# A third group of four outputs by seven products in the second SwiGLU, with the weight sums issued at listed chunks

## The chip, the cores and the metric

The kernel runs on one core of one Trainium2 chip. Its time is device time in microseconds (us) of one execution; shown are the median of several runs and, for the profile, one execution taken by the hardware profiler.

## The reference

Two decoder layers over 256 tokens of 1024 features, all in float32. Layer 0 is a short gated convolution, a cross-attention to 256 memory tokens, and a SwiGLU; layer 1 is a block-sparse causal attention that reads keys and values made once from layer 0's output, the same kind of cross-attention, and a SwiGLU. Before each part stands an RMS norm, behind each a residual sum. The change is in the SwiGLU:

```python
def swiglu(h, w_gu, w_down):
    g, u = jnp.split(h @ w_gu, 2, axis=-1)
    return (jax.nn.silu(g) * u) @ w_down
```

with h of 256 x 1024, w_gu of 1024 x 5632 and w_down of 2816 x 1024. Its 2816 outputs are worked on as 11 pairs (jp = 0 to 10) of two times 128.

## The kernel before, in words

**Precision.** Every float32 operand is split into a high and a low part (hi, lo) of a shorter type, and a product is three matmuls: hi by lo, lo by hi, hi by hi. Activations are split when they are made. Weights come from DRAM in chunks of 128 x 1024 (512 KB): a load on the SP queue into one of RAWS = 5 buffers (raw), a copy on ACT that makes hi, a subtraction on DVE that makes lo, into one of WBUFS = 10 pairs of buffers. Loads, copies and subtractions run ahead of the matmuls in one fixed order of chunks, the plan that weight_plan() returns; class Feed walks along it. A chunk's load is issued when the chunk five before it has been subtracted; its copy needs the chunk ten before it to be used up.

**The order of everything** is made when the kernel is built: PE's matmuls are written down in program order, and small jobs (generators) are put in between by a model of the engines' times (Clock, Side). The order is then fixed on each engine.

**The SwiGLU (swiglu).** The first two pairs are made by rows, the others two ways:
- A plain pair (gate_up): for each of the two outputs, gate and up are each 8 matmuls of 128 x 512 and 8 of 128 x 256 (tile gu), and ACT and DVE turn them into one output (tile guT). After each output come two blocks of the down product (tile ff, 6 matmuls each) of the pair two before.
- A group of two pairs by seven products (seven(jp), which makes jp and jp + 1). Tokens are cut into two halves, features into two halves, and gate and up are the two halves of the outputs: a 2 x 2 by 2 x 2 product. It is made by Winograd's form of Strassen's method, with seven products of 12 matmuls (tile seven) in place of eight. It needs sums over the tokens' halves (S1 to S4, made once per layer by token_sums) and sums of quarters of the weights (T1 to T4). After each product stands one block of the down product, after the last two. The results of the first token half (u0) and the second (p5) are turned by four PE transposes each (tile pt_g) and split into guT. product() takes one of two PSUM tiles for each product.

GROUPS lists the jp of the groups by layer: before, 8 in layer 0, 4 and 8 in layer 1.

**The weight sums** are made in DRAM by DMAs alone (sum_steps), 16 steps a group, two halves each: T1 is a copy of quarter B11, T3 a copy of B12, then B12 is added to T1 and B22 to T3, T2 is a copy of T1 with B22 added, T4 a copy of T2 with B21 added. Copies are issued on SP's queue, in which the weight loads stand too; additions are accumulating DMAs on GpSimd's queue (POOL), which also makes the rs (the power of -1/2) of each norm. A step waits for the one that it builds on, and whatever stands behind it in its queue waits with it. SUMS_AT says at which chunk of the plan a step is put into its queue: before, the steps of a layer were spread evenly from a first to an end chunk. In program order the chunks are, in layer 0: memv 40 to 47, mq 48 to 55, mo 56 to 63, SwiGLU 64 to 135; then k, q, v 136 to 159, memk 160 to 167, o 168 to 175, memv 176 to 183, mq 184 to 191, mo 192 to 199, and layer 1's SwiGLU from 200 on. A chunk is loaded some ten chunks before it is used.

Names in the profile: L464 is every matmul, L468 every transpose, L242 every instruction of ACT, DVE and POOL, L481 the loads, L551 and L553 the additions and the copies of the weight sums. raw_w, hi_w and lo_w are weight chunks: wr the row pairs, wg and wu gate and up of a plain pair, wB and wT quarters and sums of a group, wd the down weights; hn is a normed half of the tokens, pt_h its transposes.

Of the kernel before, what the change touches and what calls it, by code (L numbers as in the profile page):

```python
# [42 lines left out]
SPARE = 1500  # L43
LATER = 2000
BANKWISE = 5
GROUPS = ((8,), (4, 8))
SUMS_AT = ((44, 104, 104), (128, 220, 210))


class Rows:  # L50
# [18 lines left out]
def weight_plan():  # L69
# [61 lines left out]
    def ffn_plan(l):  # L131
        steps, last = ffn_steps()
        plan = []
        for kind, jp in steps + [("down", jp) for jp in last]:
            if kind == "gu" and jp in GROUPS[l]:
                plan += seven_plan(l, jp)
            elif kind == "gu" and jp - 1 in GROUPS[l] or kind == "down" and \
                    any(jp + ROW_PAIRS - g in (0, 1) for g in GROUPS[l]):
                pass
# [32 lines left out]
    for l in range(2):  # L172
        for jp in GROUPS[l]:
            for name in QUARTER:
# [224 lines left out]
def yoco_kernel(  # L399
# [22 lines left out]
    vector, scalar, pool = (Timed(clock, n, e) for n, e in  # L422
                            (("dve", nc.vector), ("act", nc.scalar), ("pool", nc.gpsimd)))
    side = Side(clock, tp=2, gu=2, half=HALVES, pair=PAIRS)
# [8 lines left out]
    def tp_tile(name):  # L433
        return ps_tp.tile([P, 4, P], F32, tag="tp", name=name)
# [21 lines left out]
    def tok(h):  # L456
        return slice(h * P, (h + 1) * P)
# [9 lines left out]
    def transpose(o, i):  # L467
        nc.tensor.transpose(o, i, ident[:i.shape[0], :i.shape[0]])  # L468
        clock.note("pe", 109, [o], [i], 200)
# [65 lines left out]
    def sum_steps(l, jp):  # L535
        for name in ("T1", "T2", "T3", "T4"):
            for i in range(2):
                weight_sums[l, jp, name, i] = aside.tile([P, 2, 2 * T], F32, name=f"{name}_{l}_{jp}_{i}")

        def step(name, source, i, add):  # L540
            dst = weight_sums[l, jp, name, i]
            if source[0] == "T":
                src = weight_sums[l, jp, source, i]
            else:
                n = quarters[l, jp, source, i]
                src = chunks[n * P:(n + 1) * P].rearrange("p (a n) -> p a n", a=2)

            def run():
                clock.free["dma"] = max(clock.free["dma"], clock.now)
                if add:  # L550
                    nc.gpsimd.dma_start(dst, src, accum_op=OP.add, max_dma_last_dim=8192)  # L551
                else:
                    nc.sync.dma_start(dst, src)  # L553
                clock.note("dma", 3300 if add else 1460, [], [])

            return run

        order = (("T1", "B11", False), ("T3", "B12", False), ("T1", "B12", True), ("T3", "B22", True),
                 ("T2", "T1", False), ("T2", "B22", True), ("T4", "T2", False), ("T4", "B21", True))
        return [step(name, source, i, add) for name, source, add in order for i in range(2)]  # L560

    plan, _, quarters, ffn_steps = weight_plan()
    feed = side.feed = Feed(clock, plan, load_chunk, split_high, split_low)
# [71 lines left out]
    def split_steps(hi, lo, pt, kind="tp"):  # L635
        scalar.copy(hi, pt)
        yield
        vector.tensor_sub(lo, pt, hi)
        side.give(kind)
        yield  # L640
# [398 lines left out]
        feed.hooks[36 + k] = [put_aside(k)]  # L1039

    for l in range(2):
        steps = [step for jp in GROUPS[l] for step in sum_steps(l, jp)]
        first, end, last = SUMS_AT[l]
        for n, step in enumerate(steps):
            at = min(first + (end - first) * n // len(steps), last + n - len(steps))
            feed.hooks.setdefault(at, []).append(step)


    def short_conv(act, into):
# [179 lines left out]
    def swiglu(l, src, done, fine_end=False, at_end=None):  # L1229
        act = src.act  # L1230
        guT = Act(side, [])

        def unit_of(j):
            if j // 4 == len(guT.units):
                guT.units.append(acts.tile([P, 4, 2, T], F32R, tag="unit", name=f"guT{l}_{j // 4}"))
            return guT.units[j // 4], j % 4
# [121 lines left out]
        def seven(jp):  # L1358

            u, j0 = unit_of(2 * jp)  # L1360
            bank_jobs, t = {}, {}
# [93 lines left out]
            def turn_parts4(src, h):  # L1455
                yield from side.hold("tp")
                pt = tp_tile("pt_g")
                for i in range(4):
                    transpose(pt[:, i, :], src[:, i * P:(i + 1) * P])
                side.give("half")  # L1460
                yield
                yield from split_steps(u[:, :, 0, tok(h)], u[:, :, 1, tok(h)], pt)

            EVICT = {"B11": b11, "B21": b21, "T1": t1, "T3": t3, "T2": t2, "B22": b22, "T4": t4}
            n = jp - ROW_PAIRS
# [17 lines left out]
                next_down()  # L1483
            next_down()
            for h, name in enumerate(("B22", "T3")):
                guT.add_job(h, jp // 2, bank_jobs[name])

        def down_w(jp):
            return [feed.take(f"wd{l}_{2 * jp + i}") for i in range(2)]
# [14 lines left out]
        steps, last = ffn_steps()  # L1504
        sums_job = [side.start(token_sums())]
        for jp in range(ROW_PAIRS, NP):
            if jp in GROUPS[l]:
                seven(jp)
# [3 lines left out]
            n = jp - ROW_PAIRS  # L1512
# [248 lines left out]
```

## Time and profile before

| | |
|---|---|
| median of 3 runs | 783.08 us (783.0 to 783.8) |
| the profiled execution | 783.51 us, of which the span from the first to the last instruction 781.7 |
| granted TensorE clock | 0.998 |
| PE busy | 773.4 us (99%), 4147 matmuls |
| DVE, ACT, POOL busy | 573.6 (73%), 458.8 (59%), 36.8 (5%) |
| moved by DMA | 182.71 MB, 234 GB/s |

Times in the trace count from the start of the span. A row of the chain gives its start, its length, and what it is; a row of a group gives how many instructions, their busy time and the mean in ns of one, then the idle time of the engine ahead of them; a row of a window gives the busy time of PE, PEld (weight loads of PE), DVE, ACT and POOL, PE's granted clock, the mean share of the 16 DMA engines, and GB/s. Layer 1's SwiGLU runs from 594.74 us to the end of the span.

### The profile page before, as it was taken

Reading aid. Unit: us, or ns where it says so; the run is one execution under the profiler, and the core shown is the slowest. Engines: PE = TensorE matmul, PEld = TensorE weight load, DVE = VectorE, ACT = ScalarE, POOL = GpSimd, SP = SyncE. Lnnn points to the kernel's source line nnn. Section 1 sums busy time; section 2 is a strip of 40 time slices with the busy share of each in tenths; the row PEclk is TensorE's granted clock in tenths of the full one; section 3 lists DMA queues with packets and bytes.
Section 4 is the critical chain, followed back from the end, with each engine's and each line's share of the span. In section 5 each row is a group of like instructions: output and inputs, shape, how many; then the busy total and the mean of one; then the engine's idle time right before and its main releaser. Section 6 shows DMA issues by size and latency. Waiting matters only on the chain.

```text
span 781.7 us, 11230 instructions
## 1 busy us (share of the span) xinstructions
PE 773.4 (99%) x4147; PEld 665.0 (85%) x4147; DVE 573.6 (73%) x872; ACT 458.8 (59%) x728; POOL 36.8 (5%) x68
## 2 busy tenths in 40 slices
PE   9999999999999999999999999999999999999996
PEld 8988888898888888888888889888988888888885
DVE  6988888768786566687766566876867876966964
ACT  6875665665654555566564563655756556655741
POOL 1000011000100000000110010030000000000000
PEclk9999999999999999999999999999999999999999
DMA  9776888916676755699787556899674646946931
GB/s 345 277 275 214 275 287 230 372 67 212 193 245 232 226 174 205 207 366 330 217 306 243 188 161 218 294 266 310 208 224 151 241 158 226 321 164 211 345 111 54
DMA packets 48807, 182.71 MB, mean 234 GB/s; under 512 B 6256, under 2 KB 7280, under 8 KB 46576
## 3 DMA queue, kind: packets, MB, share of 16 engines
q1 hardware_dynamic: 45968, 166.79, 59.7%
q0 software_dynamic: 2208, 14.68, 9.2%
q8 instruction: 32, 0.52, 0.3%
q10 hardware_dynamic: 576, 0.52, 0.2%
q14 instruction: 23, 0.19, 0.1%
HBM read 178.82 MB, written 28.31 MB: 265 GB/s over the span
## 4 chain that ended last, share of the span: by engine, by line
PE 95%; DVE 1%; issue 0%; ACT 0%; POOLq 0%; DVEq 0%; ACTq 0%
PE gu L464 17%; PE ff L464 15%; PE seven L464 7%; PE q_acc L464 6%; PE cu L464 6%; PE rows L464 6%; PE acc_mo L464 6%; PE acc_memv L464 6%; PE acc_memk L464 4%; PE pb L464 3%; PE acc_v L464 3%; PE acc_q L464 3%; PE acc_o L464 3%; PE acc_cout L464 3%; PE acc_k L464 3%; PE po L464 2%
## 5 line engine op out<-in xcount | busy, mean ns | idle before, releaser
L464 PE MATMUL ff<-hi_wd,guT 128*128 128x512 f32 (+1 forms) x352 | 108.2, 388 | 0.0
L464 PEld LDWEIGHTS ff<-hi_wd,guT 128*128 128x128 f32 x352 | 65.8, 188 | 12.8
L464 PE MATMUL ff<-lo_wd,guT 128*128 128x512 f32 (+1 forms) x176 | 68.3, 388 | 0.0
L242 DVE TENSOR_TENSOR gu_sb<-gu_sb,gu 128x256 f32<-128x256 f32 x48 | 19.9, 421 | 58.7 <-ACT gu_sb L242 58.0
L242 DVE TENSOR_TENSOR lo_wd<-raw_wd,hi_wd 128x1024 fp32r<-128x1024 f32 x44 | 53.5, 1221 | 2.9 <-ACT hi_wd L242 2.7
L242 ACT COPY gu_sb<-gu 128x256 f32<-128x256 f32 x48 | 17.8, 372 | 61.4 <-PE gu L464 61.3
L242 ACT CAST hi_wd<-raw_wd 128x1024 fp32r<-128x1024 f32 x44 | 46.1, 1050 | 11.3 <-DMA raw_wd<-in_chunks_dram 9.4
L464 PE MATMUL gu<-ffn,hi_wg 128*128 128x512 f32 x192 | 48.0, 390 | 0.0
L464 PE MATMUL gu<-ffn,hi_wu 128*128 128x512 f32 x192 | 47.6, 390 | 0.0
L464 PE MATMUL acc_memk<-mT,hi_memk 128*128 128x256 f32 x256 | 44.3, 291 | 0.0
L242 ACT CAST hi_wu<-raw_wu 128x1024 fp32r<-128x1024 f32 x32 | 33.5, 1051 | 15.2 <-DMA raw_wu<-in_chunks_dram 10.9
L464 PEld LDWEIGHTS gu<-ffn,hi_wg 128*128 128x128 f32 x192 | 35.9, 188 | 7.3
L464 PEld LDWEIGHTS gu<-ffn,hi_wu 128*128 128x128 f32 x192 | 35.8, 188 | 7.3
L464 PE MATMUL rows<-hi_wr,ffn 128*128 128x512 f32 x128 | 40.7, 395 | 0.0
L464 PE MATMUL acc_mo<-hi_mo,oT_mem 128*128 128x512 f32 x128 | 40.6, 393 | 0.0
L464 PE MATMUL acc_memv<-hi_memv,mT 128*128 128x512 f32 x128 | 39.6, 390 | 0.0
L242 DVE TENSOR_TENSOR lo_wu<-raw_wu,hi_wu 128x1024 fp32r<-128x1024 f32 x32 | 38.9, 1221 | 0.6 <-ACT hi_wu L242 0.5
L464 PEld LDWEIGHTS acc_memk<-mT,hi_memk 128*128 128x128 f32 x256 | 38.8, 199 | 0.4 <-ACT hi_memk L242 0.3
L464 PEld LDWEIGHTS ff<-lo_wd,guT 128*128 128x128 f32 x176 | 33.2, 188 | 6.2
L242 POOL TENSOR_TENSOR rs<-ms,neg_half 128x1 f32<-128x1 f32 x14 | 13.5, 964 | 436.6 <-DVE ms L242 420.2
L464 PE MATMUL q_acc<-mem,hi_mq 128*128 128x512 f32 x128 | 32.4, 394 | 0.0
L242 DVE TENSOR_TENSOR lo_wg<-raw_wg,hi_wg 128x1024 fp32r<-128x1024 f32 x24 | 28.7, 1221 | 4.0 <-ACT hi_wg L242 3.9
(277 smaller groups left out, 1954.6 us busy)
## 6 DMA issues: line engine op xcount, KB each, us to landing
raw_wd<-in_chunks_dram SPq DMA_DIRECT2D x44, 512.0 KB, 4.9
raw_wu<-in_chunks_dram SPq DMA_DIRECT2D x32, 512.0 KB, 5.0
T<-in_chunks_dram POOLq DMA_DIRECT2D x24, 512.0 KB, 7.6
raw_wg<-in_chunks_dram SPq DMA_DIRECT2D x24, 512.0 KB, 5.0
raw_wT<-T SPq DMA_DIRECT2D x24, 512.0 KB, 4.7
raw_wB<-in_chunks_dram SPq DMA_DIRECT2D x18, 512.0 KB, 5.0
raw_memv<-in_chunks_dram SPq DMA_DIRECT2D x16, 512.0 KB, 4.7
raw_mq<-in_chunks_dram SPq DMA_DIRECT2D x16, 512.0 KB, 6.0
```

The lines of the kernel that those rows point to most:

```text
L242: return call(out, *args, **kw)
L464: nc.tensor.matmul(o, l, r, start=start, stop=stop)
```

## The change

GROUPS gets three groups in layer 1, at 3, 6 and 8 (pairs 3 and 4, 6 and 7, 8 and 9; plain are 2, 5 and 10). SUMS_AT becomes a list of 16 chunks for each group, in the order of the steps. A group that begins at an odd pair has its outputs in two tiles of guT, so the last split goes in two halves, and the job that others wait for is entered under both tiles.

```diff
-GROUPS = ((8,), (4, 8))
-SUMS_AT = ((44, 104, 104), (128, 220, 210))
+GROUPS = ((8,), (3, 6, 8))
+SUMS_AT = {
+    (0, 8): (65,) * 8 + (74, 77, 81, 85, 89, 92, 96, 100),
+    (1, 3): (101, 103, 104, 106, 107, 109, 110, 111, 128, 131, 134, 137, 140, 143, 146, 149),
...
+}
@@
     for l in range(2):
-        steps = [step for jp in GROUPS[l] for step in sum_steps(l, jp)]
-        first, end, last = SUMS_AT[l]
-        for n, step in enumerate(steps):
-            at = min(first + (end - first) * n // len(steps), last + n - len(steps))
-            feed.hooks.setdefault(at, []).append(step)
+        for jp in GROUPS[l]:
+            for at, step in zip(SUMS_AT[l, jp], sum_steps(l, jp)):
+                feed.hooks.setdefault(at, []).append(step)
@@
-                yield from split_steps(u[:, :, 0, tok(h)], u[:, :, 1, tok(h)], pt)
+                if j0 == 0:
+                    yield from split_steps(u[:, :, 0, tok(h)], u[:, :, 1, tok(h)], pt)
+                    return
+                for i, v in enumerate((u, unit_of(2 * jp + 2)[0])):
+                    c, q = slice(2 - 2 * i, 4 - 2 * i), pt[:, 2 * i:2 * i + 2, :]
+                    scalar.copy(v[:, c, 0, tok(h)], q)
+                    yield
+                    vector.tensor_sub(v[:, c, 1, tok(h)], q, v[:, c, 0, tok(h)])
+                side.give("tp")
+                yield
@@
-                guT.add_job(h, jp // 2, bank_jobs[name])
+                for g in sorted({jp // 2, (jp + 1) // 2}):
+                    guT.add_job(h, g, bank_jobs[name])
```

The two groups at 6 and 8 follow each other without a plain pair in between. The steps of the group at 6 stand at chunks 159 (T1 with its additions), 166 (T3 with its additions) and 174 to 194; of the group at 8 at 168 (the copies of T1 and T3 and the additions to T1), 201 to 203 and 206 to 209.

What this moves on PE, at the third pair of layer 1. Before, behind the last down block of pair 0 (ff1_1_1 with wd1_1) stands the plain pair 3:

```order
L464 MATMUL ff1_1_1_6306<-hi_wd1_1_6208,guT1_0_6147 128x512 x2
L464 MATMUL gu_6468<-ffn1_0_6014,hi_wg1_3_0_6256 128x512 x4
L464 MATMUL gu_6468<-ffn1_1_6015,hi_wg1_3_1_6267 128x512 x4
L464 MATMUL gu_6487<-ffn1_0_6014,hi_wu1_3_0_6286 128x512 x4
L464 MATMUL gu_6487<-ffn1_1_6015,hi_wu1_3_1_6293 128x512 x4
L464 MATMUL gu_6468<-ffn1_0_6014,lo_wg1_3_0_6257 128x256 x4
L464 MATMUL gu_6468<-ffn1_1_6015,lo_wg1_3_1_6268 128x256 x4
L464 MATMUL gu_6487<-ffn1_0_6014,lo_wu1_3_0_6287 128x256 x4
L464 MATMUL gu_6487<-ffn1_1_6015,lo_wu1_3_1_6294 128x256 x4
L464 MATMUL ff1_0_0_6303<-lo_wd1_2_6439,guT1_0_6147 128x512
```

In the changed kernel the first product of the group at 3 stands there (B11 is a quarter of the weights; the rows left out repeat the two before them for the other row block of the chunk):

```order
L469 MATMUL ff1_1_1_6330<-hi_wd1_1_6232,guT1_0_6171 128x512 x2
L469 MATMUL seven_6490<-lo_wB11_1_3_0_6281,ffn1_0_6038 128x512
L469 MATMUL seven_6490<-hi_wB11_1_3_0_6280,ffn1_0_6038 128x512 x2
...
L469 MATMUL seven_6490<-lo_wB11_1_3_1_6292,ffn1_0_6038 128x512
L469 MATMUL seven_6490<-hi_wB11_1_3_1_6291,ffn1_0_6038 128x512 x2
...
L469 MATMUL ff1_0_0_6327<-lo_wd1_2_6311,guT1_0_6171 128x512
```

32 matmuls of a plain output, half of them 256 wide, have given way to 12 of 512, and the down block behind them is one instead of two.

The end of a group on PE. Before, behind the group at 4, the transposes of p5 stand after two down blocks and seven matmuls of the plain pair 6:

```order
L464 MATMUL ff1_1_1_6306<-hi_wd1_7_6714,guT1_1_6309 128x512 x2
L464 MATMUL gu_6895<-ffn1_0_6014,hi_wg1_6_0_6786 128x512 x4
L464 MATMUL gu_6895<-ffn1_1_6015,hi_wg1_6_1_6801 128x512 x3
L468 MATMUL pt_g_6907<-ident_95,p5_6720 128x128 x4
L464 MATMUL gu_6895<-ffn1_1_6015,hi_wg1_6_1_6801 128x512
```

Now there are two such ends in the middle: behind the group at 3 a plain pair follows, behind the group at 6 the first product of the group at 8 (the two pieces stand one below the other):

```order
L469 MATMUL ff1_1_1_6330<-hi_wd1_5_6589,guT1_1_6333 128x512 x2
L469 MATMUL gu_6769<-ffn1_0_6038,hi_wg1_5_0_6661 128x512 x4
L473 MATMUL pt_g_6778<-ident_95,p5_6595 128x128 x4
L469 MATMUL gu_6769<-ffn1_1_6039,hi_wg1_5_1_6676 128x512 x4
...
L469 MATMUL ff1_1_1_6330<-hi_wd1_11_7021,guT1_2_6730 128x512 x2
L469 MATMUL seven_7200<-lo_wB11_1_8_0_7094,ffn1_0_6038 128x512
L469 MATMUL seven_7200<-hi_wB11_1_8_0_7093,ffn1_0_6038 128x512 x2
...
L469 MATMUL seven_7200<-lo_wB11_1_8_1_7109,ffn1_0_6038 128x512
L473 MATMUL pt_g_7212<-ident_95,p5_7027 128x128 x4
L469 MATMUL seven_7200<-hi_wB11_1_8_1_7108,ffn1_0_6038 128x512 x2
```

The transposes behind the group at 3 have moved forward by three matmuls; behind the group at 6 seven matmuls stand ahead of them as before.

On SP's queue, the last sums of the group at 8 and the row blocks of layer 1's SwiGLU (mo1 are the last weights of the attention to memory, wr1 the row blocks). Before:

```order
L481 DMA raw_mo1_4_5489<-in_chunks_dram 128x1024
L553 DMA T2_1_8_0_513<-T1_1_8_0_511 16x8192
L481 DMA raw_mo1_5_5506<-in_chunks_dram 128x1024
L481 DMA raw_mo1_6_5550<-in_chunks_dram 128x1024
L553 DMA T2_1_8_1_514<-T1_1_8_1_512 16x8192
L481 DMA raw_mo1_7_5585<-in_chunks_dram 128x1024
...
L481 DMA raw_wr1_1_1_5876<-in_chunks_dram 128x1024
L553 DMA T4_1_8_0_517<-T2_1_8_0_513 16x8192
L481 DMA raw_wr1_1_2_5910<-in_chunks_dram 128x1024
L553 DMA T4_1_8_1_518<-T2_1_8_1_514 16x8192
```

and in the changed kernel:

```order
L486 DMA raw_wr1_0_1_5736<-in_chunks_dram 128x1024
L558 DMA T2_1_8_0_521<-T1_1_8_0_519 16x8192
L558 DMA T2_1_8_1_522<-T1_1_8_1_520 16x8192
L486 DMA raw_wr1_0_2_5798<-in_chunks_dram 128x1024
L486 DMA raw_wr1_0_3_5813<-in_chunks_dram 128x1024
L486 DMA raw_wr1_1_0_5877<-in_chunks_dram 128x1024
L486 DMA raw_wr1_1_1_5918<-in_chunks_dram 128x1024
L558 DMA T4_1_8_0_525<-T2_1_8_0_521 16x8192
L486 DMA raw_wr1_1_2_5928<-in_chunks_dram 128x1024
L558 DMA T4_1_8_1_526<-T2_1_8_1_522 16x8192
```

T4 has kept its place; T2, on which it waits, has moved back to four loads ahead of it. On GpSimd's queue the additions to T4 stand, as before, directly ahead of the two rs of the last norm.

2 rows, old and new, of the table SUMS_AT are left out of this document.

## Prediction

> **What bounds the kernel now.** I read the page's busy times and chain first, then the waits of PE, then the pieces of the chain around a group of seven products, then the windows of the stretches in which the change adds work. The page says that one engine is busy from end to end:
>
> ```profile
> span 781.7 us, 11230 instructions
> PE 773.4 (99%) x4147; PEld 665.0 (85%) x4147; DVE 573.6 (73%) x872; ACT 458.8 (59%) x728; POOL 36.8 (5%) x68
> PE 95%; DVE 1%; issue 0%; ACT 0%; POOLq 0%; DVEq 0%; ACTq 0%
> ```
>
> A busy PE alone proves little, since matmuls overlap; that it waits for nobody is told by its list of waits, which has two rows in the whole execution:
>
> ```profile
> PE warm L464 <- DVE blank L763: 1.5, 1, 1.5
> PE acc_memk L464 <- DVE lo_memk L242: 0.4, 1, 0.4
> ```
>
> So between the start and the last matmul PE is the path. Work taken off PE shortens the kernel by what it took, work added on any other engine costs nothing as long as PE still finds its operands ready. Both halves of the change can be read that way.
>
> **What the change takes off PE.** These are pieces of the chain in the second layer: one pair of outputs the plain way, the group of two pairs by seven products that begins at 651.94, and the start of the next plain pair (start, us, what).
>
> ```profile
> 635.36 5.54 PE gu L464 x32
> 640.90 2.75 PE ff L464 x12
> ...
> 651.94 2.72 PE seven L464 x12
> ...
> 678.19 0.44 PE pt_g L468 x4
> ...
> 682.79 1.59 PE gu L464 x7
> 684.38 0.44 PE pt_g L468 x4
> ```
>
> A plain pair takes 651.94 - 635.36 = 16.58 us, its down products included, so two pairs take 33.16. The group, which does the same two pairs with the same down products, takes 682.79 - 651.94 = 30.85 us with its first four transposes, and the second four (0.44) fall into the next pair: 31.29. One group more saves 33.16 - 31.29 = 1.87 us of PE time. The layer goes from five plain pairs and two groups to three plain pairs and three groups, so that is the whole gain on PE. Sums over the tokens (S1 to S4) are made once per layer already and are not made again.
>
> **What it adds elsewhere, and why I cost it at about nothing.** First the splitting of weights on ACT and DVE. A group needs 14 blocks of weights and sums and 4 down blocks, 18 in all, where two plain pairs need 12. The new order puts two groups back to back, 36 blocks in 62.6 us, one in 1.74 us. What the feed can do is seen in the group of before: its window, and the splits that DVE did in it.
>
> ```profile
> 651.90:683.30 31.40, 31.40 (x140) 25.62 (x139) 29.04 (x32) 22.61 (x25) 0.00 (x0) 1.00 0.89 318
> L242 DVE TENSOR_TENSOR lo_wT<-raw_wT,hi_wT 128x1024 fp32r<-128x1024 f32 x8 | 9.4, 1222 | 1.2 <-ACT hi_wT L242 1.2
> L242 DVE TENSOR_TENSOR lo_wd<-raw_wd,hi_wd 128x1024 fp32r<-128x1024 f32 x4 | 4.9, 1222 | 0.3 <-ACT hi_wd L242 0.3
> L242 DVE TENSOR_TENSOR lo_wB<-raw_wB,hi_wB 128x1024 fp32r<-128x1024 f32 x4 | 4.8, 1221 | 0.0
> L242 DVE TENSOR_TENSOR lo_wu<-raw_wu,hi_wu 128x1024 fp32r<-128x1024 f32 x2 | 2.4, 1222 | 0.0
> L242 DVE TENSOR_TENSOR lo_wg<-raw_wg,hi_wg 128x1024 fp32r<-128x1024 f32 x2 | 2.4, 1218 | 0.0
> ```
>
> DVE (third busy time, 29.04 of 31.40) made 8 + 4 + 4 + 2 + 2 = 20 blocks, one in 1.57 us, two more than the group used up, while PE was busy all of 31.40. Without those two DVE would be busy 29.04 - 2 x 1.22 = 26.6 us per group. Two groups in a row therefore still gain on the demand. They also start with a lead, for the blocks that the second group will need first stand where wg stands now:
>
> ```profile
> 671.84 2.35 DVE L242 TENSOR_TENSOR lo_wg<-raw_wg,hi_wg 128x1024 fp32r<-128x1024 f32 x2
> 680.07 0.69 DVE L242 TENSOR_TENSOR m<-seven,m 128x512 f32<-128x512 f32 x1
> 680.79 0.69 DVE L242 TENSOR_TENSOR p<-p,m 128x512 f32<-128x512 f32 x1
> 681.40 1.22 DVE L242 TENSOR_TENSOR lo_wd<-raw_wd,hi_wd 128x1024 fp32r<-128x1024 f32 x1
> 682.54 0.68 DVE L242 TENSOR_TENSOR p<-p,m 128x512 f32<-128x512 f32 x1
> 684.22 0.60 PE L468 MATMUL pt_g<-ident,p 128*128 128x128 f32 x4
> ```
>
> They are ready at 674.19 and wanted at 682.79, 8.6 us ahead. Cost: 0, and the bound above is the second rival.
>
> Second, the seams. The same rows show the one handover that PE takes with little to spare: after the last product p goes through four DVE rows, done at 683.22, and its transposes run at 684.22, a spare 1.0 us. PE fills that time with two down blocks and seven matmuls of the next output. At the seam between the second and third group the order keeps seven matmuls, the same spare. Behind the first group only four stand there; three fewer at 1.59 / 7 = 0.23 us each leave 0.3 us. Cost between 0 and, if one more split of 1.22 us gets in between, 0.9 + 0.2 us; I take 0.1, since the number of splits between those rows is the same in the new order. An odd first pair also makes its results land in two tiles, so an eviction of 512 columns becomes two of 256: a few tenths on ACT and DVE, far from PE's need of them (the next reader of that output comes over 8 us later, behind a gate and up of 5.54 and a down pair of 2.75).
>
> Third, the DMAs: 8 copies on SP's queue, 8 accumulations on GpSimd's, 6 loads more. The page's queues and the windows of five stretches give their price and room (second to last column: share of the 16 engines):
>
> ```profile
> q1 hardware_dynamic: 45968, 166.79, 59.7%
> q0 software_dynamic: 2208, 14.68, 9.2%
> 150.00:200.00 50.00, 50.00 (x302) 44.39 (x301) 37.23 (x66) 30.25 (x57) 0.56 (x1) 1.00 0.52 181
> 276.00:357.00 81.00, 81.00 (x404) 68.52 (x403) 57.68 (x71) 44.65 (x64) 1.56 (x2) 1.00 0.72 248
> 357.00:454.00 97.00, 96.85 (x484) 80.53 (x483) 64.43 (x116) 57.89 (x91) 6.12 (x8) 1.00 0.72 246
> 454.00:511.00 57.00, 57.00 (x374) 52.03 (x374) 41.76 (x65) 31.84 (x56) 2.59 (x4) 1.00 0.70 233
> 511.00:590.00 79.00, 79.00 (x437) 68.56 (x436) 56.21 (x89) 45.49 (x78) 8.50 (x10) 1.00 0.84 257
> ```
>
> 59.7% of 781.7 us for 166.79 MB is 2.80 us per MB, 1.47 us for a block of 0.52 MB; 9.2% for 14.68 MB is 4.90, 2.57 us a block. Eight of each make 32.3 us of all engines. By the chunks at which the sums stand, 6 copies and 8 accumulations of them fall into 276 to 511 us: 6 x 1.47 + 8 x 2.57 = 29.4 us in 235, which lifts the share from 0.715 to 0.84. The stretch from 511 to 590 runs at 0.84 today, and PE is busy in all its 79.00 us. So this too is costed at 0. Layer 0's 16 steps stay 16; the first eight now stand together at one chunk, in the stretch from about 150 to 200 us whose share is 0.52, and are through long before the norm at its end.
>
> Fourth, the queues. GpSimd also makes the rs of every norm, in order with its DMAs, and the last norm of the second layer has PE waiting close behind it:
>
> ```profile
> 576.79 0.47 SPq L553 DMA_DIRECT2D T<-T  x1
> 583.00 0.78 POOL L551 DMA_DIRECT2D T<-in_chunks_dram  x1 [3.24 <-DMA T<-T]
> 590.53 0.56 POOL L242 TENSOR_TENSOR rs<-ms,neg_half 128x1 f32<-128x1 f32 x1 [6.75 <-DVE ms L242]
> 592.23 0.60 PE L468 MATMUL pt_h<-ident,hn 128*128 128x128 f32 x4
> ```
>
> The last accumulation goes out at 583.00 and GpSimd then idles 6.75 us until ms comes. The T4 copies on SP (the second starts at 576.79) keep their places in front of the last two row blocks, and nothing more stands on GpSimd between them and rs than today. What moves is T2 of this group, from among the mo blocks to behind the second row block: its copies, its accumulations and then T4 must follow in the time of four loads instead of seven to nine. I expect T4 to start within 2 us of where it does, inside the 6.75. Cost 0.
>
> **Sum.** The profiled execution took 783.51 us, 1.81 around its span. 783.51 - 1.87 + 0.1 = 781.7; its distance to the median of the runs shown, 783.08, is 0.43, so I forecast a median of 781.3. The smallest difference that I count, 0.2%, is 1.57 us, about what a measurement of this kernel can tell from no change; the gain of 1.77 is only just over it.
>
> **The rivals.**
> *The gain is eaten at seams* (0.26). Several spares are small: the 0.3 us behind the first group, 1.0 at the other seams, and the denser sums just ahead of the attention's output blocks. One split of 1.22 us in the wrong place at both new seams costs 1.1, two loads late by a landing's spread cost another. With 0.3 to 3.4 us lost the time is 781.5 to 784.6, inside 0.2% of before; middle 782.4. For it: the spares are small and a kernel with no waits has nowhere to hide one. Against: the order keeps the number of splits in each.
> *The two groups in a row starve PE* (0.06), slower than before. Place: third group, its T blocks. If a block takes s us instead of 1.57, PE stops for 36 x (s - 1.74) - 8.6 us, above zero from s = 1.98; it outweighs the gain and 1.57 more from s = 2.07. At s = 2.1 it is 4.4 us: 783.08 - 1.87 + 4.4 = 785.6. Loads go round in five buffers, so that means each landing 2.5 us later. For it: the DMA share in the group's window is 0.89 already. Against: 20 blocks were made at just that share.
> *The last norm comes late* (0.05). If the chain T2, T4 slips by x us, PE stops for x - 6.75; slower by 1.57 from x = 10.2; at x = 12 it loses 5.25, which gives 786.5. Accumulations do spread:
>
> ```profile
> L551 POOL DMA_DIRECT2D T<-in_chunks_dram x24: 778/812/1382, 126.7 to 583.0; - x24
> DMA to landing us min/median/max: 3.1/5.8/12.3
> 596.84 1.39 POOL L242 TENSOR_TENSOR rs<-ms,neg_half 128x1 f32<-128x1 f32 x1 [5.75 <-DVE ms L242]
> ```
>
> With 12.3 us for two steps of that chain instead of the median 5.8, x would be 13; against it, that is the longest landing of all these DMAs, and two would have to meet. GpSimd itself is not steady: its rs took 0.56 us once and 1.39 another time, an issue 778 to 1382 ns. Eight issues more at the longest excess are 8 x 0.6 = 4.8 us on an engine that is idle 95%, spread over 300 us, so only the two before rs count. The Trainium skill, "SBUF — State Buffer", section "Who interferes with whom", speaks against eight more such DMAs: one that looks stalled by a VectorE instruction was issued from GpSimd, whose writing of descriptors was kept from a port it shares with VectorE, while an instruction of VectorE with two inputs in SBUF, such as a split, holds up only what GpSimd reads. The rows agree in size (0.8 us at the longest, less than one split), and show no DMA starved for long; taken at its worst the rule would double this rival's chance.
> *It isn't done as said* (0.03): a wait that I have not seen at a spot where sums now stand in a burst, four copies and two accumulations at once ahead of the output blocks. That gives anything from 782 to 785 and is in the range below.
>
> **How the numbers follow.** Forecast 0.60: 781.0 to 781.5 (1.87 plus the small run-to-run step of about 0.1 on one side, 0.3 lost on the other). Faster by over 0.2%, below 781.5: 0.60 from it and 0.01 from the first rival. Within 0.2%: the rest of that rival and half of the unseen waits, 0.27. Slower, over 784.65: 0.12. The range takes the forecast whole and the nearer two thirds of the first rival: 780.9 to 783.2, which leaves some 0.2 outside, nearly all above.
>
> **What would show it.** Right: PE's list of waits still has only the two rows of the start, three groups of about 31.3 us, and the second layer's part from its first plain pair to the end shorter by 1.9. Seams: a PE row that waits for p or guT beside a group. Starving: PE <- lo_wT or lo_wB in the third group. Norm: rs with no idle before it, or PE waiting for hn about 590 us. Wrong altogether: PE idle over 0.5 us in any window from 30 to 770 us, or a group over 32 us.

## The result and the profile after

The changed kernel takes 792.83 us (median of 5 runs, 791.27 to 795.94) against 783.08 (782.98 to 783.88): ratio 1.0125, 95% interval 1.0101 to 1.015. It is slower by 9.75 us where 1.8 us of gain were forecast.

On the page of the profiled execution (792.05 us) PE has 36 matmuls fewer, but it holds only 84% of the chain of work that ended last, before 95%; DMA has 5% of it, DVE 4%. The two queue rows show what was added.

```profile
span 790.3 us, 11186 instructions
...
PE 776.5 (98%) x4111; PEld 661.8 (84%) x4111; DVE 581.3 (74%) x875; ACT 461.7 (58%) x726; POOL 43.6 (6%) x76
...
q1 hardware_dynamic: 47088, 174.13, 61.4%
q0 software_dynamic: 2848, 18.88, 11.5%
...
PE 84%; DMA 5%; DVE 4%; ACT 2%; issue 1%; POOL 0%; POOLq 0%; DVEq 0%; ACTq 0%; SPq 0%
```

Where the time went is read from the starts of the stages. For each kind of matmul the rows below give the number, the duration (least, median, most), and the start of the first and of the last; kernel before first, then after.

```profile
L464 PE MATMUL rows<-lo_wr,ffn x64: 387/389/483, 200.8 to 617.7; 128*128 128x512 f32 x64
L464 PE MATMUL acc_k<-lo_k,moba x32: 389/389/478, 384.4 to 407.4; 128*128 128x512 f32 x32
L464 PE MATMUL acc_o<-hi_o,oT_moba x64: 389/389/482, 491.2 to 513.5; 128*128 128x512 f32 x64
L464 PE MATMUL q_acc<-mem,lo_mq x128: 277/283/364, 146.1 to 566.6; 128*128 128x256 f32 x128
L464 PE MATMUL acc_mo<-hi_mo,oT_mem x128: 387/389/485, 173.0 to 594.5; 128*128 128x512 f32 x128
```

```profile
L469 PE MATMUL rows<-lo_wr,ffn x64: 387/390/504, 200.1 to 627.4; 128*128 128x512 f32 x64
L469 PE MATMUL acc_k<-lo_k,moba x32: 387/389/476, 385.5 to 408.1; 128*128 128x512 f32 x32
L469 PE MATMUL acc_o<-hi_o,oT_moba x64: 387/389/481, 491.9 to 518.4; 128*128 128x512 f32 x64
L469 PE MATMUL q_acc<-mem,lo_mq x128: 277/283/368, 145.4 to 575.2; 128*128 128x256 f32 x128
L469 PE MATMUL acc_mo<-hi_mo,oT_mem x128: 387/389/498, 172.3 to 604.1; 128*128 128x512 f32 x128
```

After minus before: -0.7 at layer 0's SwiGLU (first rows), +1.1 at k, +0.7 at the first o, +4.9 at the last o, +8.6 at the end of mq, +9.6 at the end of mo, +9.7 at the last rows, and +8.6 at the end of the span. So layer 0's SwiGLU loses 1.8, the attention's o stage 4.2, memv and mq 3.7, mo 1.0; the layer with the third group gains, as meant, though 1.1 in place of 1.77. Finer figures below, such as 1.7 at o1, compare in the same way the first matmul on each chunk of weights (o1, v1, mq1 and so on are the weights of layer 1's stages).

The windows of three of the stretches costed in the prediction, and of the worst 27 us among them:

```profile
357.00:454.00 97.00, 97.00 (x486) 80.87 (x485) 67.82 (x119) 57.12 (x91) 8.74 (x10) 1.00 0.81 266
454.00:511.00 57.00, 56.59 (x366) 50.13 (x365) 37.49 (x59) 27.55 (x48) 3.68 (x5) 1.00 0.81 256
511.00:590.00 79.00, 74.52 (x405) 63.92 (x405) 53.77 (x87) 45.55 (x80) 7.71 (x8) 0.98 0.81 262
525.00:552.00 27.00, 25.04 (x119) 20.67 (x118) 16.25 (x23) 13.35 (x18) 4.28 (x5) 1.00 1.00 313
```

The mean share is 0.81 in all three stretches, close to the 0.84 forecast for 276 to 511, and yet PE does 405 matmuls in the last one where it did 437. Inside it the share is 1.00 for 27 us. The next rows are PE's longest waits behind the start (us in total, times, longest), with the longest in the list of its weight loads, PEld; then comes the chain through the first of them (start, us, what):

```profile
PE s L469 <- ACT q L247: 1.9, 1, 1.9
PE pt_h L473 <- DVE x_sb L247: 1.7, 1, 1.7
...
PEld acc_o L469 <- DVE lo_o L247: 2.6, 6, 0.7
```

```profile
535.27 13.37 DMA raw_mo<-in_chunks_dram
...
548.73 1.05 ACT hi_mo L247
549.78 0.28 ACT q_sb L247
...
550.08 0.43 DVE q_sb L247
...
550.54 0.41 ACT q L247
...
550.97 0.44 DVE q L247
...
551.45 1.55 PE s L469 x8
```

A load of mo1_0 takes 13.37 us to land. ACT's next instruction is its copy; q_sb, for which PE waits, stands behind it, although PE wants mo1_0 only at 575. **No weight is missing here: the engine that would serve PE is held up by a load that nobody needs yet.** The Trainium skill, "Perfetto Trace Analysis", section "Tensor Engine Instruction (MATMUL, LD_WEIGHTS)", says that ACT and DVE take their instructions strictly in order; these rows agree.

The wait is only half of what is lost there. Behind it PE's granted clock was 0.50 from 552.11 to 555.52 us; in the profile of before it falls nowhere between 8 and 778 us. The rows give that window, then the twelve matmuls of s before and after, and five of q_acc in the slow stretch and behind it:

```profile
552.11:555.52 3.41, 3.41 (x13) 2.99 (x12) 3.38 (x5) 1.06 (x2) 0.00 (x0) 0.50 0.73 279
```

```profile
544.92 1.59 PE L464 MATMUL s<-memk_u,q 128*128 128x256 f32 x12
...
550.99 2.65 PE L469 MATMUL s<-memk_u,q 128*128 128x256 f32 x12 [1.88 <-ACT q L247]
553.44 2.28 PE L469 MATMUL q_acc<-mem,hi_mq 128*128 128x512 f32 x5
...
560.35 1.41 PE L469 MATMUL q_acc<-mem,hi_mq 128*128 128x512 f32 x5
```

The matmuls in that stretch took some 1.9 us longer (1.06 and 0.87), so the wait and the slower clock together make 3.8 of the 4.0 us lost at mq. Why the clock fell is not shown: behind a wait of 3.13 us in the run e1_unbooked it did not.

At o1 it is otherwise: there the weights are late. PE's own list has only 0.2 us of it; the waits stand in the list of PEld (2.6 us for lo_o), because ACT copied the first chunk 11.45 us behind its landing, 1.12 before.

This second kind of loss stands at layer 0's row blocks too. Two of ACT's copies there, before and after (start, us for both):

```profile
176.67 2.00 ACT L242 CAST hi_wr<-raw_wr 128x1024 fp32r<-128x1024 f32 x2
```

```profile
195.27 1.99 ACT L247 CAST hi_wr<-raw_wr 128x1024 fp32r<-128x1024 f32 x2
```

Before, these are the first and the second chunk; after, the second and the third (the first is copied at 175.96). The load of the second chunk landed at 176.61 before and was copied 1.01 us later; after, it landed at 178.40 and was copied 16.87 us later, at 195.27. Its copy stands 17 us later in ACT's order. The planner books each sum on its own model of the DMA (3300 ns an addition, 1460 a copy, one behind the other), and the eight steps at chunk 65 put that model 19 us behind, so it writes the copy there.

### The profile page after: what moved, and what is told of

Its sections match the earlier page's. It is cut to its first block, busy times and chain, and to the rows that moved or that the text cites. A ratio compares the mean times of both kernels' runs of the same rounds, so it can differ in the third digit from the quotient of the medians.

```text
span 790.3 us, 11186 instructions
## 1 busy us (share of the span) xinstructions
PE 776.5 (98%) x4111; PEld 661.8 (84%) x4111; DVE 581.3 (74%) x875; ACT 461.7 (58%) x726; POOL 43.6 (6%) x76
## 3 DMA queue, kind: packets, MB, share of 16 engines
q0 software_dynamic: 2848, 18.88, 11.5%
## 4 chain that ended last, share of the span: by engine, by line
PE 84%; DMA 5%; DVE 4%; ACT 2%; issue 1%; POOL 0%; POOLq 0%; DVEq 0%; ACTq 0%; SPq 0%
PE ff L469 14%; PE gu L469 14%; PE seven L469 8%; PE cu L469 6%; PE acc_mo L469 5%; PE q_acc L469 5%; PE acc_memv L469 4%; PE rows L469 4%; PE acc_memk L469 3%; PE pb L469 3%; PE acc_v L469 3%; PE acc_q L469 3%; PE acc_k L469 3%; PE acc_cout L469 3%; PE s L469 2%; PE po L469 2%
## 5 line engine op out<-in xcount | busy, mean ns | idle before, releaser
L247 DVE TENSOR_TENSOR gu_sb<-gu_sb,gu 128x256 f32<-128x256 f32 x40 | 16.5, 419 | 41.6 <-ACT gu_sb L247 41.5
L556 POOL DMA_DIRECT2D T<-in_chunks_dram x32 | 25.4, 821 | 343.8 <-DMA T<-T 199.9
L247 DVE TENSOR_TENSOR lo_wT<-raw_wT,hi_wT 128x1024 fp32r<-128x1024 f32 x32 | 38.1, 1221 | 4.1 <-ACT hi_wT L247 4.0
L469 PE MATMUL gu<-ffn,hi_wg 128*128 128x512 f32 x160 | 40.1, 391 | 0.0
L247 ACT CAST hi_wT<-raw_wT 128x1024 fp32r<-128x1024 f32 x32 | 32.9, 1052 | 12.1 <-DMA raw_wT<-T 10.5
L469 PE MATMUL gu<-ffn,hi_wu 128*128 128x512 f32 x160 | 39.6, 390 | 0.0
L247 ACT CAST hi_wu<-raw_wu 128x1024 fp32r<-128x1024 f32 x28 | 29.4, 1051 | 15.7 <-DMA raw_wu<-in_chunks_dram 14.0
L247 DVE TENSOR_TENSOR lo_wu<-raw_wu,hi_wu 128x1024 fp32r<-128x1024 f32 x28 | 33.9, 1219 | 1.8 <-ACT hi_wu L247 1.8
L469 PEld LDWEIGHTS gu<-ffn,hi_wg 128*128 128x128 f32 x160 | 29.7, 188 | 6.4 <-DVE gu_sb L247 0.5
L469 PEld LDWEIGHTS gu<-ffn,hi_wu 128*128 128x128 f32 x160 | 29.8, 188 | 6.1
```

The lines of the kernel that those rows point to most:

```text
L247: return call(out, *args, **kw)
L469: nc.tensor.matmul(o, l, r, start=start, stop=stop)
```

## The experiments

Each series ran beside the kernel before (783.44 to 783.84 us there); a time stands with its ratio to that and the 95% interval.

**1. Which half: the booking, the transfers, or the groups.**

`e1_unbooked`, the sums not booked in the model:

```diff
-                clock.note("dma", 3300 if add else 1460, [], [])
```

> The changed kernel with all its DMAs, but the weight sums are no longer booked on the planner's model of the DMA (3300 ns an addition, 1460 a copy, one after the other). Theory A, the booked steps: eight or six steps booked at one chunk put the model's DMA some 20 us behind, so the planner writes the copies of weights that have long landed far back in ACT's order (hi_wr0_0_1 starts 16.87 us behind its landing, in the kernel before 1.01; hi_o1_0 11.45 against 1.12), and the loads behind them go out late. Then this kernel loses most of the 9.75 us: 781 to 784, and hi_wr0_0_1 and hi_o1_0 start within 2 us of their landing. Rival B, the transfers themselves (landings of 8 to 13 us between 495 and 552 us, 4 to 6 before): 790 or more, with the same long landings. Rival C, the third group itself: 790 or more.

792.31, 1.0114 (1.0098 to 1.013). The copies came where theory A wanted them (0.02 us behind the landing for wr0_0_1, 1.01 for o1_0), o1 lost nothing, and yet the time stayed: the loss moved to layer 0's last down blocks (2.6 us), to v1 (3.3) and to mq (2.5). At v1 the chain reads as above:

```profile
427.60 9.31 DMA raw_v<-in_chunks_dram
...
437.01 1.15 ACT hi_v L247
438.16 0.58 ACT r L247
...
439.80 0.63 PE pt_r L473 x4
```

Theory A falls as the whole cause.

`e2_booked_no_sums`, booked, but no DMA of the sums issued:

```diff
-                if add:
-                    nc.gpsimd.dma_start(dst, src, accum_op=OP.add, max_dma_last_dim=8192)
-                else:
-                    nc.sync.dma_start(dst, src)
```

> The changed kernel with the sums still booked in the planner's model at the same chunks, but none of their 64 DMAs issued; the T loads read plain quarters of the weights instead (the products of the groups are thus made with other numbers). Theory A: still slow, at least the first losses in the order's own places stay (about 1.5 us at the row pairs of layer 0, 1.75 us at the attention's output blocks o1) and some of what follows from loads issued late: 784 to 790. Rival B: with the transfers gone nothing is late, 781.2. Rival C: 790 or more.

785.85, 1.0031 (1.0018 to 1.0043). The booking alone keeps 3.5 us over the next run, at the row blocks (1.1), o1 (1.6) and mo1.

`e3_groups_alone`, neither booking nor DMAs:

> Three groups in the second layer, with neither the DMAs of the sums nor their booking; the T loads read plain quarters (other numbers in the products). Theories A and B: what the third group is worth by itself, 783.08 - 1.87 = 781.2, give or take 0.5, and no PE row idle over 0.5 us. Rival C, the groups cost more than they save (seams, splits): 784 or more, with PE waiting beside the groups.

782.38, 0.9983 (0.9974 to 0.9991). Rival C falls; three groups are worth 1.3 us by the ratio (0.7 to 2.0). This run leaves out the sums of the old groups too, so that some of the 1.3 may be theirs.

`e4_bursts_two_groups`, the groups of before with the new list:

```diff
-GROUPS = ((8,), (3, 6, 8))
+GROUPS = ((8,), (4, 8))
-    (1, 3): (101, 103, 104, ...
+    (1, 4): (101, 103, 104, ...
```

> The groups of before (4 and 8), with the new list of chunks: the sums of layer 0 as in the change (eight at chunk 65), those of group 4 where the change has group 3, those of 8 as in the change (six at chunk 168). Bursts without the third group. Theories A and B: slower than before by 3 to 8 us, 786 to 791, with PE waiting for row blocks of layer 0 near 200 us and for o1 near 490 us. Rival C: as before, 783 give or take 0.5.

786.85, 1.0047 (1.0035 to 1.006). The list alone costs two groups 3.7 us. The third group's further steps make it 9.75, its gain already taken off.

**2. Copies or additions; bursts or amount.**

`e8_copies_only`, the additions left out:

```diff
-                    nc.gpsimd.dma_start(dst, src, accum_op=OP.add, max_dma_last_dim=8192)
+                    pass
```

> The change, booked as it is, with the 32 additions on GpSimd's queue left out (T1 to T4 are then plain copies, so other numbers go into the products). Which of the two DMAs holds the weight loads up? If the additions: as with no sums at all but booked, 785.5 to 787. If the copies that stand on SP's queue among the loads: 790 or more. In between: both, by their share of the engines' time (copies 1.47 us, additions 2.57) it would be some 788.

786.5, 1.0034 (1.0022 to 1.0046): 0.65 us over the run without any sums. The copies cost little; with the booking in place the additions carry the other 6 us. Layer 1's loads of memv and mo land in 5.0 and 4.4 us (medians) where the change has 8.6 and 7.4, and the kernel before 4.3 and 5.6.

The next three place the same DMAs otherwise. `e5_three_even`:

```diff
+    (0, 8): (44, 47, 51, 55, 59, 62, 66, 70, 74, 77, 81, 85, 89, 92, 96, 100),
+    (1, 3): (104, 106, 108, 110, 112, 115, 117, 119, 121, 123, 126, 128, 130, 132, 134, 137),
+    (1, 6): (139, 141, 143, 145, 148, 150, 152, 154, 157, 159, 161, 163, 165, 168, 170, 172),
+    (1, 8): (174, 176, 179, 181, 183, 185, 187, 190, 192, 194, 196, 198, 201, 203, 205, 207),
```

> Three groups with all their sums, booked as always, but no two steps at one chunk: layer 0's at the chunks of before (44 to 100), the 48 of layer 1 one after the other from 104 to 207, about one each 2.2 chunks. The same work and the same DMAs as in the change, other places. Theory D (the bursts: booked at one chunk they move the copies back, and their transfers meet the loads that then go out late): nearly all of the 9.75 us goes, and with the 1.2 us that three groups alone are worth in this series it is 782 to 783.5. Rival E (the amount: 8 copies and 8 additions more are too much wherever they stand): 786 or more, with PE waiting at a DMA between 380 and 590 us.

789.59, 1.0076 (1.0064 to 1.0087). Theory D falls: without any burst 6 us are lost, nearly all in layer 0's group and last pair (6.5 us between 344 and 379).

`e6_layer0_even` (the (0, 8) row of e5 alone):

> The change, with layer 0's 16 steps at the chunks of before, the first eight no more together at chunk 65. Theory D: what is lost at the row pairs of layer 0 goes (1.1 us between the first and the last of the wr chunks, 0.55 at wd0_0), and the rest stays: 790.5 to 791.5, with wr0_1_0 used as early as in the kernel before. Rival E: no more than 0.5 us, 792 to 793.

789.61, 1.007 (1.0057 to 1.0082). Layer 0 and the change's steps for group 3 then lose nothing, up to o1; the losses from o1 on are those of the change (1.6, 1.8, 4.5, 1.1). This is 3.2 us less than the change, more than either theory gave the burst.

`e7_late_two_even`:

```diff
+    (1, 6): (153, 154, 156, 158, 160, 161, 163, 165, 167, 169, 170, 172, 174, 176, 177, 179),
+    (1, 8): (181, 183, 185, 186, 188, 190, 192, 193, 195, 197, 199, 201, 202, 204, 206, 208),
```

> The change, with the 32 steps of the groups at 6 and 8 spread from chunk 153 to 208, none two at one chunk, instead of standing at 159, 166 and 168. Layer 0 and group 3 as in the change. Theory D: the losses from o1 on (1.74 at o1, 2.09 up to memv1, 4.03 at mq1, 1.1 at mo1, in the profiles) mostly go: 784 to 787. Rival E: 789 or more, since the transfers in that stretch are as many.

790.12, 1.0085 (1.0073 to 1.0097). o1 loses 0.9 and mq 1.1 instead of 1.7 and 4.0, but v1 now loses 3.1. As with e5, a loss goes where the steps go.

**3. Is there a good place?** Theory F: where the feed has slack.

`e9_third_early`, `e10_third_as_changed` and `e11_third_half_early` keep all steps of before at their chunks and add group 3's (in this order):

```diff
+    (1, 3): (66, 68, 70, 73, 75, 78, 80, 83, 85, 87, 90, 92, 95, 97, 100, 102),
+    (1, 3): (101, 103, 104, 106, 107, 109, 110, 111, 128, 131, 134, 137, 140, 143, 146, 149),
+    (1, 3): (66, 71, 76, 81, 86, 91, 96, 101, 128, 131, 134, 137, 140, 143, 146, 149),
```

> Three groups with all their sums. The steps of layer 0 and those of the groups at 6 and 8 stand at the very chunks of the kernel before (44 to 100, and 128 to 209 for its two groups); the 16 of the group at 3 are put between them at chunks 66 to 102, in layer 0's plain pairs, and none from 103 to 127, where layer 0's own group is fed. Theory F (not how many and not only the bursts, but where: additions cost where the feed has little lead and the engines are near full, as around layer 0's group and from v1 to mq1, and are free elsewhere): no PE wait that the kernel before does not have, 782 to 783 (before less the 1.2 to 1.5 of the third group). Rival E (8 copies and 8 additions more are too much wherever they stand): 786 or more.

> As the kernel just described, but the steps of the group at 3 at the change's own chunks: 101 to 111 (eight, around the feed of layer 0's group) and 128 to 149 (between the others). Theory F: the eight at 101 to 111 cost nothing by themselves, as in the run with layer 0's steps alone spread; from 128 to 149 two groups' steps share 22 chunks, so additions run at twice the rate of before there, ahead of v1: 783 to 787, with PE waiting at q1, v1 or k1. Rival E: 786 or more.

> As the first of these three, but only the first eight steps of the group at 3 early (chunks 66 to 101, one in five) and the last eight at 128 to 149 with those of the group at 6. Theory F: layer 0 as in the kernel before, a wait at q1 or v1 as in the second of the three, 782.5 to 786. Rival E: 786 or more.

794.37 (1.0128, 1.0115 to 1.0142), 791.07 (1.0092, 1.0079 to 1.0105), 786.34 (1.0038, 1.0023 to 1.0053). Theory F is wrong in its first run, by 11 us: plain pairs have room, but not for 16 steps on top of those that stand there. In e9 PE waits 3.7 us at 222.70, where ACT is held up by a load of wd that takes 11.08 us; then the share is 0.99 from 240 to 276, and PE loses another 6 us between 280 and 318. In e10 the chain runs through one load of 15.18 us:

```profile
361.76 15.18 DMA raw_wd<-in_chunks_dram
...
376.97 1.05 ACT hi_wd L247
...
378.04 1.23 DVE lo_wd L247
379.27 0.34 DVE gu_sb L247
...
380.09 0.41 ACT guT L247
...
380.55 3.49 PE ff L469 x8
```

Again something that PE wants, guT, stands in the engines' order behind the copy and the split of a late load. Only e11, with the steps thinnest, comes near.

**4. Early copies or late loads.** Theory G: it is only the order, so copies written further back would free ACT.

`e12_planned_later`, `e13_half_early_later` (on e11), `e14_before_later` and `e16_layer0_even_later` (on e6): the model takes each load of a weight as landed 4000 ns later, from chunk 64 on.

```diff
-        clock.note("dma", (1.55 if rows else 1.9) * math.prod(dst.shape[1:]), [dst], [], 900)
+        clock.note("dma", (1.55 if rows else 1.9) * math.prod(dst.shape[1:]), [dst], [], 900 + later)
```

> The change with all its DMAs at its own chunks; only the planner's model takes every weight load from chunk 64 on as landed 4000 ns later than it did, so the copies of weights stand further back in ACT's order. Theory G (head of line: the engines hold the loads up by 10 to 15 us, ACT's next instruction is the copy of such a load, and behind it stand the small steps for which PE waits at once, as q_sb behind hi_mo1_0, whose block PE wants only 27 us later): the waits for q, x_sb and gg go, the two losses of the booked bursts (1.1 and 1.7 us) stay: 784 to 788. Rival H (the weights themselves come too late, the engines have not the room): 791 or more, with PE waiting for lo blocks.

> Three groups, the sums as in the run that put the first half of group 3's at chunks 66 to 101, and the model's landing 4000 ns later from chunk 64 on. Theory G: its waits of 1 us each behind a wd load and at q1 and v1 go, leaving the 1.2 to 1.8 of the third group as a gain: 781 to 783.5. Rival H: as without the later landing, 786, or more.

> A control: the kernel before, unchanged but for the model's landing taken 4000 ns later from chunk 64 on. Theories G and H both: nothing waits there, so no more than 0.5 us either way, 783 to 784. If it gains by itself, the two runs beside it have to be read against it.

> As the run with layer 0's steps at the chunks of before and the rest as in the change (789.6), with the model's landing 4000 ns later from chunk 64 on. Theory G: the waits at memv1 and mq1 (1.75 and 4.6 us there) go, the burst's 1.5 at o1 may stay: 782.5 to 785. Rival H: 789 or more.

801.94 (1.0232, 1.0218 to 1.0246), 803.65 (1.0257, 1.0243 to 1.0271), 788.89 (1.0068, 1.0054 to 1.0081), 798.49 (1.0187, 1.0173 to 1.0201). Theory G's remedy is worse than the ill, even on the kernel before (5.3 us, where at most 0.5 was expected). PE's waits in e12:

```profile
PE ff L469 <- DVE lo_wd L247: 5.7, 4, 2.2
PE seven L469 <- DVE lo_wB L247: 3.2, 5, 1.8
```

The wait for q is gone although mo1_0 still takes 13.34 us to land, so that wait did come from the order on ACT. But a load goes out only when the chunk five before it is subtracted: copies further back make every load later, and now the weights themselves run out. **Too early a copy stops ACT, too late a copy starves PE; the longer a landing takes, the less is left between the two.**

**5. The lead itself**, that is how far the loads run ahead of the copies and the matmuls. `e17_by_room` fills each stretch only as far as the engines have time there; `e18_seven_raw` leaves the change as it is and gives the loads two buffers more; `e19_before_seven_raw` does the same to the kernel before.

```diff
+    (0, 8): (44, 47, 51, 55, 59, 62, 65, 67, 69, 71, 73, 75, 78, 81, 82, 83),
+    (1, 3): (66, 70, 84, 86, 89, 97, 101, 105, 107, 110, 113, 144, 146, 148, 150, 151),
+    (1, 6): (153, 155, 158, 160, 160, 161, 161, 162, 162, 163, 163, 164, 164, 165, 177, 180),
+    (1, 8): (182, 186, 190, 196, 200, 201, 202, 203, 204, 205, 206, 207, 208, 208, 209, 209),
```

```diff
-RAWS = 5
-WBUFS = 10
+RAWS = 7
+WBUFS = 9
```

> Three groups with all their sums, each stretch of eight chunks given only as many steps as it has room for. Room, from the run without sums: the time between the issues of its first and last load, less eight loads at 1.47 us; a copy takes 1.47 of it and an addition 2.57. By this count the change fills the stretch 168 to 175 to 1.95 and 128 to 135 to 1.16, the even spread 112 to 143 to between 1.12 and 1.45, the early one 88 to 103 to 1.14 and 1.08: each above 1 where PE later stopped. Here none that takes any step is above 0.89 (120 to 127 and 168 to 175 take none). Theory I (a stretch filled beyond its room delays the loads, from which ACT stops or the weights run out): 781.5 to 784, the third group's gain with at most 1.5 us of it lost. Rival J (additions slow the loads behind them wherever they stand, room or not): 787 or more.

> The change with seven buffers for loads in place of five, paid for with nine pairs of split blocks in place of ten. Theory I: the engines are what is full at 168 to 175, and more loads under way do not make them faster, but two loads more lie ready when it comes: part of the loss goes, 786 to 791. Rival K (five loads under way are too few once a landing takes over 10 us, 5 in 10 + 2.3 + waits being one in 2.8 us where PE uses one in 2.76): most of it goes, 782 to 786. If 792 or more: the order of the copies decides and not the lead.

> The kernel before with seven buffers for loads and nine pairs of split blocks: the control for the run that did the same to the change (782.7, 0.9989 of before). Theory I (the lead of five loads is what the change used up; before had enough of it): 783 to 784, so that the third group, with its sums at the change's own bursts, is worth 0.5 to 1.5 us once the lead is there. Rival L (the buffers help any version of this kernel): 782 or less, and the third group is then worth nothing.

e17: 784.33, 1.0013 (1.0004 to 1.0023), the best of the eight placements of three groups with five buffers and the planner's model as it was, a little over its forecast and 2 us over the groups alone. The count of room is a guide and not a law: the change's own stretch of 1.16 (chunks 128 to 135) lost nothing.

e18: **782.70, 0.9989 (0.998 to 0.9997): the change with its own bursts loses nothing more, and is 0.9 us under the kernel before** (less than the 1.57 us that the prediction counts as a difference). e19: 784.76, 1.0014 (1.0005 to 1.0023), so the buffers are no gain by themselves. The 79 us ahead of layer 1's SwiGLU in e18, the 27 us in which the change stood at share 1.00, and the loads there (KB each, median us to landing):

```profile
511.00:590.00 79.00, 79.00 (x437) 68.56 (x436) 56.23 (x89) 45.68 (x78) 7.76 (x9) 1.00 0.84 263
525.00:552.00 27.00, 27.00 (x144) 23.19 (x143) 19.83 (x31) 16.96 (x27) 0.33 (x1) 1.00 1.02 331
```

```profile
T<-in_chunks_dram POOLq DMA_DIRECT2D x10, 512.0 KB, 8.2
raw_memv<-in_chunks_dram SPq DMA_DIRECT2D x8, 512.0 KB, 10.3
raw_mo<-in_chunks_dram SPq DMA_DIRECT2D x8, 512.0 KB, 9.9
```

The engines are as full as in the change and the landings longer, yet PE loses nothing: 437 matmuls in the stretch, as before. What differs is that the feed, the sums included, runs two chunks further ahead. The load of memv1_2 is issued at 485.22 instead of 499.55 and has landed 8.28 us before its copy, in the change 0.10. That of mo1_0 is issued at 529.47 instead of 535.27; ACT still stands 1.79 us before its copy, but at 540.09 instead of 548.73, and PE has no wait for what comes behind it. **The added transfers, the additions above all, make landings long, and five loads of lead did not cover them; seven do.** The two runs with more buffers also have one pair of split blocks less, and the planner orders the copies anew for them, so what is shown is the lead together with the order that goes with it.

## Why the prediction was wrong, step by step

- **PE's gain of 1.87 a group: right.** It lies within what was measured, 1.1 to 2.0. From the last rows block to the end of the span: 164.0 us before, 162.9 after, 1.1 less, where 1.77 were forecast. With seven buffers in both kernels, e18 against e19 gives 0.9989 / 1.0014 = 0.9975, 2.0 us.
- **The feed of back-to-back groups: right.** None of the change's listed waits is for lo_wT or lo_wB; e3 runs three groups from five buffers at 782.38.
- **The seams: at most 0.8 in place of 0.1** (1.87 less the 1.1). From start to start (start, us, what) the group at 6 takes 724.01 - 692.92 = 31.09 against 30.85, with transposes of 0.66 for 0.44; the rest I have not placed:

```profile
692.92 2.72 PE seven L469 x12
...
719.17 0.66 PE pt_g L473 x4
...
724.01 1.59 PE seven L469 x7
```

- **The last norm: right.** T4's additions go out at 590.30 and 592.77, and rs follows with 6.61 us to spare (6.75 before). Here the norm itself came over 9 us late; in e18, where it did not, the last addition goes out at 580.79 and rs has 8.98 us to spare. The rows of the change:

```profile
592.77 0.78 POOL L556 DMA_DIRECT2D T<-in_chunks_dram  x1 [1.70 <-DMA T<-T]
600.16 0.56 POOL L247 TENSOR_TENSOR rs<-ms,neg_half 128x1 f32<-128x1 f32 x1 [6.61 <-DVE ms L247]
```

- **"Third, the DMAs ... costed at 0": the step that failed.** The price of the DMAs was right (11.5% of the engines' time for 18.88 MB, 4.8 us per MB, 4.9 forecast), and so, nearly, was the mean share (0.81 for 0.84). The inference was wrong: that a stretch at 0.84 with PE busy proves room for others to reach 0.84. What decides is whether a single load lands within the lead of five, and a mean over 80 us does not show that. The row that should have warned was in the profile of before:

```profile
525.00:552.00 27.00, 27.00 (x143) 23.19 (x143) 18.85 (x31) 16.77 (x27) 1.56 (x2) 1.00 0.94 305
```

  PE is busy there, but the engines are nearly full: what is added has to come out of the lead.
- **Layer 0's first eight steps, "through long before the norm at its end": true of the transfers, wrong for the kernel.** The eight steps moved 17 us of ACT's order through the planner's booking, which I had read in the code and not priced (1.1 us there by e2; in the same run o1, behind the six steps at chunk 168, loses 1.6).
- **The rivals.** None had this mechanism at this size. The nearest, the unseen wait at a burst (0.03, 782 to 785), had the place and a third of the price.

What stays open: how the 9.75 us divide between copies written too late and copies held up, since both draw on the same lead (booking alone 3.5, transfers without booking 9.9, both together 10.4 over the groups alone); why the stretch of 1.16 was free; and what made the clock fall behind the wait for q. The prediction's own test for "wrong altogether", PE idle over 0.5 us in a window, came true from 511 to 590. Its first sign, PE's list of waits, would have missed o1, where the waits stand under PEld.

## What to carry to other kernels

Do not cost a transfer at nothing because the mean share leaves room: take the longest landing that the added transfers will make, and compare it with what the loads' buffers cover, stage by stage. Where an engine with a fixed order splits or copies what arrives, a late load stops everything behind it, so look at what stands behind that copy, not only at when its result is wanted. And when a change costs more than it should, test the slack (one buffer more) before the placement: eight placements were tried here, and two buffers took the loss away.

## What the runs showed of the hardware

- An accumulating DMA of 0.52 MB from DRAM to DRAM takes 8.1 us to land (median of 32), and holds up loads on another queue: layer 1's loads of mo land in a median of 7.4 us in the change, and in 4.4 in e8, where only the additions are left out. The Trainium skill, "DMA: Bandwidth & Descriptors", section "Queues, rings and completion order", says that each DMA engine serves its queues in turn, packet by packet; the medians fit that, though no row shows the turns themselves.
- A single load of 0.52 MB landed in 3.1 us where the engines were idle ahead of it (o1_0 before, at 473.45); in e10 one took 15.18 us, with three additions and a copy issued within 1 us of it.
- Behind a wait of 1.88 us PE's granted clock was 0.5 for 3.41 us, so that the wait cost about twice its length.
